# The first mixer's normalised input multiplied on VectorE instead of GpSimd, and 17 zero matmuls instead of 14 at the start

## The chip, the core and the metric

The kernel runs on one core of a Trainium2 chip. A core has five engines with a queue of instructions each: TensorE for matrix products (its weight loads are shown as a row of their own), VectorE, ScalarE and GpSimd for element-wise work, and SyncE, whose queue here issues DMAs. Each engine works through its queue in order and waits on semaphores for the others. The metric is the time of one execution on the device in microseconds (us); lower is better.

## The reference, cut to what matters

Two layers of a streaming encoder run over 320 tokens: 256 of a new stream and 64 of a running one. Layer 0 is a Mamba-2 mixer and a ConvFFN, layer 1 is an attention mixer and a ConvFFN. The change touches the way into the mixer of layer 0:

```python
def rmsnorm(x, g):
    xf = x.astype(F32)
    y = xf * lax.rsqrt(jnp.mean(xf * xf, axis=-1, keepdims=True) + EPS)
    return (y * g.astype(F32)).astype(x.dtype)

def mamba2_mixer(h, conv_buf, ssm_state, w_in, conv_w, conv_b, ...):
    zxbcdt = h @ w_in
    z, xbc, dt = jnp.split(zxbcdt, [D_INNER, D_INNER + CONV_DIM], axis=-1)
    xbc_c, new_buf = causal_dwconv(xbc, conv_buf, conv_w, conv_b)
    xbc_c = jax.nn.silu(xbc_c)
...
h = rmsnorm(x, norm_mix_pre[layer])
mix = mamba2_mixer(h, ...)
```

Here `x` has 1024 channels, and `w_in` is a 1024 x 5152 matrix. All numbers are float32.

## The kernel before, in words

**Layout.** Channels lie on the 128 partitions and the 320 tokens on the free axis, so `x` is eight tiles of 128 x 320, called k-blocks 0 to 7 here. One output block of a projection is 128 output channels: it is summed over the eight k-blocks in one PSUM bank.

**Three products for one.** Each float32 operand is split into a high part (rounded to the TensorE's fp32r type, on ScalarE) and a low part (the rest, on VectorE). A product is three matmuls: high by high, high by low, low by high (`mm3`, L279 and L280). A triple of them below means one k-block of one output block. Weights are split the same way as they arrive: `wh` on ScalarE (L322, L325), `wl` on VectorE (L324, L326); both have rings of four buffers.

**Scaling early or late.** The norm's factor of a token, 1/sqrt(mean square), is known only when all of `x` has been squared and summed. So the first output blocks multiply the unnormalised `x * g`, split into `xgh` and `xgl`, and their results are multiplied by the factor afterwards. These are four blocks in `outer` (the first one is `dt`, the other three go to convolutions 0, 1 and 2) and three more in the loop `for i in range(3, 3 + RAW0)` (convolutions 3, 4 and 5; "raw blocks" 3, 4, 5 below). From then on every block multiplies the normalised input, split into `xnh` and `xnl`.

**The normalised input.** `normalized` returns eight steps, one for each k-block. A step multiplies `x[:, k, :]` by the factor (`xr`, spread over the partitions) on GpSimd (L478), and splits the result `xn`, with the gain, on ScalarE (`xnh`, L325) and VectorE (`xnl`, L326). The tile `xn` has two buffers, so step k + 2 can start when both readers of step k are done. Three steps stand in the program behind raw block 3, three behind raw block 4, two behind raw block 5.

**What holds PSUM.** In this part the pool `pm` has four banks (`PSM`, m=4). The block `dt` gives its bank back when L815 has multiplied it by the factor; each convolution block gives its bank back when L642 has multiplied it by the factor into `ext`. Both run on VectorE. The tile `ext` has three buffers; a buffer comes free when the three taps of its convolution (L649, VectorE) and the copies of its last columns (L643 and L644, GpSimd) have been done. The first normalised block takes the fourth bank; the second one takes the bank of raw block 3, and so on.

**Zero matmuls.** `busy` (L375) issues matmuls of zeros whose result nothing reads; `run` issues `WARM` of them at L617, before any weight has arrived.

**Order.** In this part nobody writes the order by hand. The tile framework runs its own estimate of durations over the program (`schedule_with_timeline_sim=True`, L1515) and puts each engine's instructions into a fixed queue: what is ready first in its estimate goes first, and among several that are ready the one that stands earlier in the program. The chip then follows these queues whatever the true durations are.

Of the kernel before, what the change touches and what calls it, by code (L numbers as in the profile page):

```python
# [12 lines left out]
ALU = mybir.AluOpType  # L13
# [13 lines left out]
# the mixer of layer 0: projections, and how many steps of the scan and of the gate go with each block of them  # L27
# [6 lines left out]
WARM = 14  # L34
BA, BB = (14, 14, 14, 0), (10, 10, 10, 0)
AHEAD = 1, 2
# what is split before each of the three boundaries: units of the ring, units in a pool of their own; high parts right past it
# [8 lines left out]
# of 1 / sqrt(u), u from 0.932 to 1.07: over w = RSU * u, (w * w + RS[0] * w + RS[1]) * (w * w + RS[2] * w + RS[3])  # L46
# [35 lines left out]
class Kern:  # L82
# [132 lines left out]
    def ahead(self, i, cap=None):  # L215
        """loads and splits for the units after i; until the boundary is passed, two of the next phase's at most"""
        if cap is None:
            cap = self.ends[0] + RING[3 - len(self.ends)] if self.ends else len(self.q)
        while True:
            if self.qd < min(len(self.q), i + self.LD + 1, self.qs + 3):  # L220
                self._dma(self.qd)
                self.qd += 1
            elif self.qs < min(self.qd, i + self.LS + 1, cap):
                self._split(self.qs)()
                self.qs += 1
            else:
                return

    def early_open(self):
        """the weights of a phase that are loaded and split in the phase before, in a pool of their own"""  # L230
        early = self.early[3 - len(self.ends)]
        self.est = ExitStack()
        pool = self.pool(self.est, "early", "right")
        self.eready = []
        raws = []

        def load(src, n):
            raws.append(self.t(self.wp, [P, 1024], "wr", bufs=3))
            self.nc.sync.dma_start(out=raws[-1][:, :n], in_=src)

        def split(n, g):
            h, l = (self.t(pool, [P, n], f"e{c}{n}", F32R, bufs=sum(e[1] == n for e in early)) for c in "hl")
            r = raws.pop(0)
            for c0, c1, sc in g or ((0, n, None),):
                self.split(h[:, c0:c1], l[:, c0:c1], r[:, c0:c1], sc)
            self.eready.append((h, l))

        loads = [lambda u=u: load(*u[:2]) for u in early]
        splits = [lambda u=u: split(*u[1:]) for u in early]
        if loads:  # L250
            loads.pop(0)()
        return [(loads.pop(0) if loads else None, f) for f in splits]
# [8 lines left out]
    def high_ahead(self, n):  # L261
        """past the boundary: the high parts of the next units, and the low ones for later"""
        self.lows = []
        for _ in range(n):
            self.ahead(self.wi, self.qs)
            self.lows.append(self._split(self.qs))
            self.qs += 1
# [26 lines left out]
    def psum(self, **n):  # L294
        """the eight banks, by use"""
        if self.pst is not None:
            self.pst.close()
        self.pst = ExitStack()
        self.psp = {}
        for k, b in n.items():  # L300
            p = self.pst.enter_context(self.tc.tile_pool(name=self.nm("ps" + k), bufs=b, space=PSUM, reuse_waits="tile"))
            self.psp[k] = p
# [15 lines left out]
    def split_high(self, hdst, ldst, src, scale=None, pool=False):  # L318
        """the high part of src (by scale), and what makes the low one"""
        nc = self.nc  # L320
        if scale is None:
            self.high_ins = nc.scalar.activation(out=hdst, in_=src, func=AF.Copy).ins  # L322
            e = nc.gpsimd if pool else nc.vector
            return lambda: e.tensor_tensor(out=ldst, in0=src, in1=hdst.bitcast(F32), op=ALU.subtract)  # L324
        nc.scalar.activation(out=hdst, in_=src, func=AF.Copy, scale=scale)  # L325
        return lambda: nc.vector.scalar_tensor_tensor(out=ldst, in0=src, scalar=scale, in1=hdst.bitcast(F32),  # L326
                                                      op0=ALU.mult, op1=ALU.subtract)
# [4 lines left out]
    def newton(self, v, pool, tag):  # L332
        """1 / sqrt(v) of a few columns: a seed from the exponent, and a polynomial of fourth degree in v * seed ** 2"""
# [15 lines left out]
    def mean(self, src, dim, pool):  # L349
        """src / dim + eps"""  # L350
        v = self.t(pool, [P, 3], "nwv", bufs=3)
        self.nc.vector.tensor_scalar(v, src, 1.0 / dim, EPS, op0=ALU.mult, op1=ALU.add)
        return v

    def toksum(self, acc, ps, o=0):
        """sums over the channels, tokens on partitions: three columns (the last block twice)"""
        mm = self.nc.tensor.matmul
        one = self.ones[:, 0:1]
        for b in range(2):
            mm(ps[:, o + b:o + b + 1], acc[:, b * 128:b * 128 + 128], one, start=True, stop=True)  # L360
        for p0 in (0, 64):
            i = mm(ps[p0:p0 + 64, o + 2:o + 3], acc[:, 256:320], one, start=True, stop=True)
        self.pe_end = i.ins

    def spread(self, r, ps=None):
        """[tokens on partitions, 3] to every partition, tokens on the free axis (PSUM)"""
# [5 lines left out]
    def busy(self, ps, n, w=256):  # L372
        """matmuls of zeros, into columns that nothing reads: the array's clock drops when it rests for some microseconds"""
# [17 lines left out]
    def late_rstd(self):  # L391
        """of the eight output blocks: the sum of seven is there before the eighth"""
# [14 lines left out]
    def enter(self, xgp, sp, tag, g=None, boundary=True):  # L407
        """closes the residual of the layer before and splits x * g (block 0: x), channel block by block;
        sums the squares of x"""
# [60 lines left out]
    def normalized(self, xgp, sp, g, rstd):  # L470
        """x * rstd * g, in eight steps"""
# [4 lines left out]
        def step(k):  # L476
            xn = self.t(sp, [P, T], "xn", bufs=2)
            nc.gpsimd.tensor_tensor(out=xn, in0=self.x[:, k, :], in1=rstd, op=ALU.mult)  # L478
# [43 lines left out]
    def square_part(self, xh, xl, kbs, ps, mid, nstop):  # L522
        """a part of the sum of four output blocks of a 2048 x 1024 product, K outermost, two K blocks a unit"""
# [9 lines left out]
    def square_first(self, xh, xl, groups, ps, mid=None):  # L533
        """the first four output blocks of a 2048 x 1024 product, K outermost"""
# [27 lines left out]
    def outer_part(self, ps, ks, xh, xl, behind=None, turned=False):  # L562
        """K blocks of several output blocks; turned: block by block"""
# [14 lines left out]
    def outer(self, nblk, xh, xl, xacc, pool):  # L578
        """the first blocks of a projection, K outermost, and 1 / sqrt of the mean square of x"""
# [49 lines left out]
    def conv(self, ps, rstd, pool, k, pads, w, b, rows_out, dst=None):  # L629
        """k-tap depthwise conv along the tokens of both streams; returns (taps sum, ext)"""  # L630
# [22 lines left out]
    def after(self, ins, *earlier):  # L653
        """issue order alone"""
# [3 lines left out]
    def table(self, func):  # L658
        """has the table of a function loaded before it is waited for"""
# [13 lines left out]
    def ssm(self):  # L673
# [3 lines left out]
        with ExitStack() as st:  # L677
# [3 lines left out]
            with ExitStack() as s2:  # L681
# [4 lines left out]
                with ExitStack() as s3:  # L686
# [17 lines left out]
                    xnh, xnl, steps = self.normalized(xgp, dp, "mix_pre0", rstd)  # L704
# [97 lines left out]
    def ssm_dt(self, ps, rstd, sp, dp):  # L802
        """dt = softplus(.) and the sums of dt * a along a chunk; chunks and heads on partitions, tokens of a chunk on the free axis"""
# [60 lines left out]
    def ssd_select(self, g, sp):  # L864
        """X, of a pair of heads of the group and zero elsewhere, for the four pairs"""
# [4 lines left out]
    def ssd_decay(self, g, sp):  # L870
        """exp(acs_l - acs_s) under the causal mask, and exp(acs) by channel, of the heads of a group"""
# [136 lines left out]
    def ffn(self, i):  # L1008
        nc, a = self.nc, self.a
        with ExitStack() as st:  # L1010
# [3 lines left out]
            with ExitStack() as s2:  # L1014
# [9 lines left out]
                xnh, xnl, steps = self.normalized(xgp, sp, f"ffn_pre{i}", rstd)  # L1024
# [39 lines left out]
    def mla(self):  # L1064
        nc, a = self.nc, self.a
        tt, ts, stt = nc.vector.tensor_tensor, nc.vector.tensor_scalar, nc.vector.scalar_tensor_tensor
        with ExitStack() as st:
# [10 lines left out]
            with ExitStack() as s2:  # L1078
# [28 lines left out]
                # the norm of a projection of the normalized x, of its sums over the unscaled x: r / sqrt(mean * r * r + eps),  # L1107
                # r = 1 / sqrt(vx), is 1 / sqrt(mean + eps * vx)
# [80 lines left out]
    def turn_rope(self, sp, ps):  # L1189
        """the turned parts of two heads, of each the high rows and (in the rows of the other) the low ones; of the second the sample's tokens first"""  # L1190
# [32 lines left out]
    def attend(self, kp, sp, ql, kk, ch, cl, cqh, cql, sc, oh, ol, u):  # L1223
# [6 lines left out]
        def scores(qlh, qll, qs):  # L1230
            pt = self.t(sp, [P, 2, 3, 128], "pt", bufs=1)
            pss = self.t(sp, [P, T], "pss", bufs=2)
            for qb in range(3):
                ps = self.px()
                if qb == 0:
                    # the two parts of the keys side by side, their products added after
# [148 lines left out]
def _blocks(w):  # L1385
    """(K, N) to (N/128, 128, K/128 * 128): per output block, K rows on partitions"""
# [4 lines left out]
def _outer(w, nb):  # L1391
    """the first nb output blocks, K outermost: (8, 128, nb * 128)"""
# [3 lines left out]
def _square(w):  # L1396
    """(2048, 1024) to units in the order of use: 2 K blocks by 4 output blocks, then 8 K blocks of one"""
# [122 lines left out]
```

## Time and profile before

| what | value |
|---|---|
| median of the runs | 1015.43 us |
| lowest and highest of three runs | 1014.97 and 1017.46 us |
| span of the profiled execution | 1015.3 us |
| TensorE busy (matmul) | 987.5 us, 97% |
| VectorE busy | 753.6 us, 74% |
| ScalarE busy | 612.3 us, 60% |
| GpSimd busy | 352.3 us, 35% |

Only the span of the profiled execution is given, from its first to its last instruction; it lies 0.1 us under the median of the runs, so what lies around the span is smaller than the spread of the runs. In the rows of the profile PE is TensorE's matmuls, PEld its weight loads, DVE VectorE, ACT ScalarE, POOL GpSimd and SP SyncE. `L478` is line 478 of the kernel. In a timeline row the two first numbers are the start and the duration in us, and square brackets hold the idle time of that engine just before and the instruction that ended it.

### The profile page before, as it was taken

The page shows a single profiled execution, that of the slowest core. Times are in us where ns is not written, and L with a number is a line of the kernel's source. Part 1 is how long each engine was busy: PE and PEld are TensorE (multiplying, and loading weights), DVE is VectorE, ACT ScalarE, POOL GpSimd, SP SyncE. Part 2 cuts the span into 40 slices and gives each one's busy share as a digit, 9 for nine tenths or more (in the row PEclk, how much of TensorE's full clock was granted, in tenths as well). Part 3 has the DMA queues.
Part 4 walks back from the last instruction along what each step waited for, and adds up shares of the span by engine and source line. Part 5 has one row for each costly group of instructions (what it writes and reads, how often), then busy time and mean ns, then how long its engine had stood idle before and what let it go on. Part 6 is the DMA issues. An engine that isn't in the chain of part 4 may idle for free.

```text
span 1015.3 us, 18255 instructions
## 1 busy us (share of the span) xinstructions
PE 987.5 (97%) x6679; PEld 941.0 (93%) x6679; DVE 753.6 (74%) x1418; ACT 612.3 (60%) x1269; POOL 352.3 (35%) x601
## 2 busy tenths in 40 slices
PE   8999999999999999999999999999999999999995
PEld 7998888889988999999998899989999999999995
DVE  7896879767577999785447898886547999876333
ACT  7575777754455678665445487675545678665330
POOL 4832323000015676440005565640003667442001
PEclk9999999999999999999999999999999999999998
DMA  7352323233324344445641222232451444444441
GB/s 257 109 175 88 133 94 129 94 119 125 130 63 155 135 161 154 146 145 195 193 144 47 75 81 64 65 104 75 149 161 59 150 167 166 146 149 151 149 117 52
DMA packets 42664, 128.70 MB, mean 127 GB/s; under 512 B 4880, under 2 KB 8528, under 8 KB 42576
## 3 DMA queue, kind: packets, MB, share of 16 engines
q1 hardware_dynamic: 42288, 127.22, 37.9%
q8 instruction: 52, 0.85, 0.3%
q14 instruction: 36, 0.29, 0.1%
q10 hardware_dynamic: 288, 0.33, 0.1%
HBM read 123.46 MB, written 4.07 MB: 126 GB/s over the span
## 4 chain that ended last, share of the span: by engine, by line
PE 86%; DVE 8%; POOL 2%; issue 2%; ACT 1%; DMA 0%; DVEq 0%; POOLq 0%; ACTq 0%
PE pm L279 49%; PE pm L280 24%; PE px L279 2%; PE px L943 1%; PE px L960 1%; PE px L280 1%; DVE wl L324 1%; PE pb L886 1%; PE px L951 1%; POOL xacc L442 1%; PE pr L360 1%; POOL xn L478 1%; DVE y L450 1%; DVE x L454 1%; PE px L926 1%
## 5 line engine op out<-in xcount | busy, mean ns | idle before, releaser
L324 DVE TENSOR_TENSOR wl<-wr,wh 128x1024 fp32r<-128x1024 f32 (+2 forms) x204 | 246.8, 1210 | 119.5 <-ACT wh L322 114.4
L322 ACT ACTIVATE wh<-wr 128x1024 fp32r<-128x1024 f32 (+4 forms) x235 | 228.0, 973 | 163.5 <-PE pm L279 148.3
L279 PE MATMUL pm<-xnh,wh 128*128 128x320 f32 x784 | 244.7, 313 | 2.1 <-ACT xnh L325 1.8
L279 PE MATMUL pm<-xnl,wh 128*128 128x320 f32 x784 | 244.4, 312 | 0.3 <-DVE xnl L326 0.3
L280 PE MATMUL pm<-xnh,wl 128*128 128x320 f32 x784 | 244.3, 312 | 0.0
L279 PEld LDWEIGHTS pm<-xnh,wh 128*128 128x128 f32 x784 | 147.7, 189 | 5.8 <-issue 2.7
L280 PEld LDWEIGHTS pm<-xnh,wl 128*128 128x128 f32 x784 | 147.7, 189 | 3.5 <-issue 3.2
L279 PEld LDWEIGHTS pm<-xnl,wh 128*128 128x128 f32 x784 | 147.8, 189 | 3.2 <-issue 2.3
L279 PE MATMUL pm<-ah,wh 128*128 128x320 f32 x452 | 140.2, 311 | 0.0
L280 PE MATMUL pm<-ah,wl 128*128 128x320 f32 x452 | 140.1, 311 | 0.0
L279 PE MATMUL pm<-al,wh 128*128 128x320 f32 x452 | 139.9, 310 | 0.0
L649 DVE SCALAR_TENSOR_TENSOR cv<-ext,vec,cv 128x322 f32<-128x322 f32 x176 | 97.5, 568 | 5.5 <-ACT cv L647 3.0
L643 POOL COPY fsave<-ext 128x2 f32<-128x2 f32 x88 | 72.2, 821 | 53.8 <-ACT ext L640 49.3
L279 PEld LDWEIGHTS pm<-ah,wh 128*128 128x128 f32 x452 | 84.8, 188 | 1.2 <-ACT wh L322 0.8
L280 PEld LDWEIGHTS pm<-ah,wl 128*128 128x128 f32 x452 | 84.8, 188 | 0.5 <-issue 0.4
L279 PEld LDWEIGHTS pm<-al,wh 128*128 128x128 f32 x452 | 84.9, 188 | 0.1
L324 POOL TENSOR_TENSOR wl<-wr,wh 128x512 fp32r<-128x512 f32 (+2 forms) x31 | 43.5, 1418 | 103.6 <-ACT wh L322 100.6
L636 POOL MEMSET ext<- 128x2 f32 (+1 forms) x112 | 10.9, 98 | 188.7 <-PE px L943 55.9
L280 PE MATMUL pm<-xgh,wl 128*128 128x320 f32 x220 | 68.2, 314 | 0.7 <-DVE wl L326 0.7
L279 PE MATMUL pm<-xgl,wh 128*128 128x320 f32 x220 | 68.2, 313 | 0.3 <-DVE xgl L426 0.3
L279 PE MATMUL pm<-xgh,wh 128*128 128x320 f32 x220 | 63.1, 319 | 2.9 <-ACT xnh L325 1.4
L442 POOL TENSOR_TENSOR xacc<-xacc,xsq 128x320 f32<-128x320 f32 x28 | 29.2, 1043 | 104.3 <-ACT xsq L441 103.8
(424 smaller groups left out, 2200.7 us busy)
## 6 DMA issues: line engine op xcount, KB each, us to landing
wr<-w_up SPq DMA_DIRECT2D x76, 512.0 KB, 3.2
wr<-w_in SPq DMA_DIRECT2D x37, 512.0 KB, 3.3
wr<-w_dn SPq DMA_DIRECT2D x32, 512.0 KB, 3.5
wr<-w_out SPq DMA_DIRECT2D x16, 512.0 KB, 3.2
wr<-w_o SPq DMA_DIRECT2D x16, 512.0 KB, 3.2
wr<-w_up_k SPq DMA_DIRECT2D x16, 384.0 KB, 3.0
wr<-w_dn SPq DMA_DIRECT2D x16, 384.0 KB, 3.1
wr<-w_uq SPq DMA_DIRECT2D x8, 384.0 KB, 3.1
```

What stands on the lines that cost most here:

```text
L279: for i in (mm(out, wh, xh, start=first, stop=False), mm(out, wh, xl, start=False, stop=False), mm(out, wl, xh, start=False, stop=last)):
L280: mm(out, wl, xh, start=False, stop=last)):
L322: self.high_ins = nc.scalar.activation(out=hdst, in_=src, func=AF.Copy).ins
L324: return lambda: e.tensor_tensor(out=ldst, in0=src, in1=hdst.bitcast(F32), op=ALU.subtract)
L360: mm(ps[:, o + b:o + b + 1], acc[:, b * 128:b * 128 + 128], one, start=True, stop=True)
L442: nc.gpsimd.tensor_tensor(out=acc, in0=acc, in1=s, op=ALU.add)
L450: tt(out=yk, in0=yk, in1=r, op=ALU.mult)
L454: e.tensor_tensor(out=xk, in0=xk, in1=yk, op=ALU.add)
L478: nc.gpsimd.tensor_tensor(out=xn, in0=self.x[:, k, :], in1=rstd, op=ALU.mult)
L636: nc.gpsimd.memset(ext[:, 0:m], 0.0)
L643: nc.gpsimd.tensor_copy(out=rows_out[:, 0, :], in_=ext[:, TP:TP + m])
L649: nc.vector.scalar_tensor_tensor(out=c, in0=ext[:, i:i + n], scalar=w(i), in1=c, op0=ALU.mult, op1=ALU.add)
```

## The change

Two edits change what is computed where; the others in the diff take comments out.

```diff
-WARM = 14
+WARM = 17
...
-    def normalized(self, xgp, sp, g, rstd):
+    def normalized(self, xgp, sp, g, rstd, e):
...
-            nc.gpsimd.tensor_tensor(out=xn, in0=self.x[:, k, :], in1=rstd, op=ALU.mult)
+            e.tensor_tensor(out=xn, in0=self.x[:, k, :], in1=rstd, op=ALU.mult)
...
-                    xnh, xnl, steps = self.normalized(xgp, dp, "mix_pre0", rstd)
+                    xnh, xnl, steps = self.normalized(xgp, dp, "mix_pre0", rstd, nc.vector)
...
-                xnh, xnl, steps = self.normalized(xgp, sp, f"ffn_pre{i}", rstd)
+                xnh, xnl, steps = self.normalized(xgp, sp, f"ffn_pre{i}", rstd, nc.gpsimd)
```

In the first layer's mixer all eight multiplications of `x` by the factor go to VectorE. The two ConvFFNs keep theirs on GpSimd. `run` issues 17 zero matmuls instead of 14.

## The prediction

> **What bounds the kernel now.** I read the page first: its span, the busy shares and the row of slices.
>
> ```profile
> span 1015.3 us, 18255 instructions
> PE 987.5 (97%) x6679; PEld 941.0 (93%) x6679; DVE 753.6 (74%) x1418; ACT 612.3 (60%) x1269; POOL 352.3 (35%) x601
> PE   8999999999999999999999999999999999999995
> ```
>
> TensorE (PE) is busy nearly all the time, so a microsecond comes off the total only where PE stands still or runs slowly, and from there a gain is carried to the end as long as no later wait takes it back. The first two slices (25 us each) hold the first mixer's entry. Next I read the chain of work that ended last, for the first 60 us (start, us, what).
>
> ```profile
> 27.22 1.77 issue
> ...
> 29.01 3.73 issue
> 32.74 0.53 POOL ssave L644
> 33.27 1.67 POOL xn L478 x2
> ...
> 35.36 4.13 POOL xn L478
> ...
> 39.52 0.57 ACT xnh L325
> ...
> 40.13 1.16 PE pm L279 x3
> ```
>
> From 27 to 40 us the chain runs through GpSimd (POOL): a copy of three columns, then the steps that the change moves, then `xnh`, and only then PE. The timeline of that stretch shows why, and what PE does meanwhile.
>
> ```profile
> 27.09 5.70 POOL L643 COPY ssave<-ext 128x3 f32<-128x3 f32 x1
> 38.05 0.31 PE L280 MATMUL pm<-xnh,wl 128*128 128x320 f32 x1
> 40.13 0.90 PE L279 MATMUL pm<-xnh,wh 128*128 128x320 f32 x2 [1.77 <-ACT xnh L325]
> 41.09 0.47 PE L280 MATMUL pm<-xnh,wl 128*128 128x320 f32 x1
> 41.36 0.47 PE L279 MATMUL pm<-xnh,wh 128*128 128x320 f32 x1
> 43.76 0.37 PE L279 MATMUL pm<-xnh,wh 128*128 128x320 f32 x1
> ```
>
> A copy of 128x3 took 5.70 us, while VectorE (DVE) had no gap. The tile view gives the moved instruction the same spread:
>
> ```profile
> L478 POOL TENSOR_TENSOR xn<-x,xr x8: 870/946/4124, 23.0 to 43.0; 128x320 f32<-128x320 f32 x8
> ```
>
> Alone it takes 0.87 us, at worst 4.12. The Trainium skill, page "SBUF — State Buffer", section "SBUF: two separate sides", says that GpSimd and a VectorE instruction with two SBUF inputs exclude each other for a whole instruction; these rows agree with it.
>
> PE waited 1.77 us at 38.3 and then ran at half speed: 0.27 us from one matmul to the next (41.09 to 41.36) until 43.76. The windows view (window, length, then busy us and count of PE, PEld, DVE, ACT, POOL, then PE's granted clock, DMA share and GB/s) gives the full pace and the load of VectorE.
>
> ```profile
> 22.00:48.00 26.00, 22.78 (x141) 21.99 (x140) 22.71 (x49) 14.69 (x25) 22.09 (x25) 0.93 0.41 142
> 25.80:36.40 10.60, 10.60 (x72) 10.60 (x73) 9.09 (x23) 5.45 (x9) 9.51 (x9) 1.00 0.43 151
> 36.40:43.76 7.36, 5.59 (x28) 5.23 (x26) 5.64 (x12) 4.29 (x8) 7.33 (x14) 0.78 0.21 73
> ```
>
> 72 matmuls in 10.60 us are 0.147 us each: three raw blocks without a gap. In the third window PE did 25 (28 less three at the edges), which need 25 x 0.147 = 3.7 us; 3.7 of 7.4 us are lost there.
>
> **The change part by part.**
>
> *Taking `xn` off GpSimd.* Gone are eight instructions and the wait for them, and one stretched weight split:
>
> ```profile
> 21.89 1.08 DVE L324 TENSOR_TENSOR wl<-wr,wh 128x896 fp32r<-128x896 f32 x1
> 22.95 2.69 POOL L478 TENSOR_TENSOR xn<-x,xr 128x320 f32<-128x320 f32 x2 [5.13 <-ACT xr L388]
> 23.16 1.76 DVE L324 TENSOR_TENSOR wl<-wr,wh 128x896 fp32r<-128x896 f32 x1
> 24.84 0.81 DVE L815 TENSOR_TENSOR v<-pm,xr 32x128 f32<-32x128 f32 x3
> 25.80 0.39 PE L279 MATMUL pm<-xgh,wh 128*128 128x320 f32 x1 [1.45 <-ACT xnh L325]
> ```
>
> The same split takes 1.08 us alone and 1.76 beside `xn`. Behind it stands L815, which frees the PSUM bank that raw block 3 needs; the profile names `xnh` as releaser, but the block reads no `xnh`, and L815 ends at 25.65. So raw block 3 can start 0.68 us earlier, and the raw blocks end at about 35.75 instead of 36.43.
>
> *Putting it on VectorE.* The nearest row is a two-input instruction of the same shape; the pitch in a full queue comes from two neighbours.
>
> ```profile
> 5.10 0.48 DVE L429 TENSOR_TENSOR xgl<-x,xgh 128x320 fp32r<-128x320 f32 x1
> 35.34 0.54 DVE L649 SCALAR_TENSOR_TENSOR xs<-ext,vec,xs 128x323 f32<-128x323 f32 x1
> 35.80 0.54 DVE L326 SCALAR_TENSOR_TENSOR xnl<-xn,vec,xnh 128x320 fp32r<-128x320 f32 x1
> ```
>
> 0.46 us from start to start: eight steps are 8 x 0.46 = 3.7 us. In 22 to 48 us VectorE had 26.0 - 22.7 = 3.3 us free, and 0.68 us more comes from the split above: the steps fit, with almost nothing over. What matters is what they are put ahead of. Behind them stand the low parts `xnl`, the weight splits, the `dt` arithmetic, the convolution taps, and L642, which empties the banks:
>
> ```profile
> 34.73 0.55 DVE L326 SCALAR_TENSOR_TENSOR xnl<-xn,vec,xnh 128x320 fp32r<-128x320 f32 x1 [1.51 <-ACT xnh L325]
> 39.76 0.54 DVE L642 TENSOR_TENSOR ext<-pm,xr 128x256 f32<-128x256 f32 x2
> 45.07 0.54 DVE L642 TENSOR_TENSOR ext<-pm,xr 128x256 f32<-128x256 f32 x2
> ```
>
> L642 at 39.76 gives back the bank of raw block 3 at B = 40.30. The second normalised block needs it. PE reaches it when the first normalised block is done: 35.75 + 24 x 0.147 = 39.3. So once `xn` is no longer late, the next thing that is late is this bank. Before it VectorE had one gap of 1.51 us. The inputs of `xn` are complete at 22.9, before anything that the raw blocks bring, so I let all eight stand ahead of L642. Then B = 40.30 + 3.7 - 1.51 - 0.68 = 41.8. The four `xnl` that came after it before may move ahead too: 4 x 0.46 = 1.8 more, B = 43.6. If the planner puts L642 no later than now, B = 40.3 or less. I take 41.8, the middle one, since two steps may be in flight at a time and `xnl` waits for ScalarE in between.
>
> *What it is worth.* Before, PE had done 25 normalised matmuls by 43.76. After, it has done 24 by B and goes on at 0.147 us. The gain is therefore (43.76 - B) - 0.147, if the clock holds: 1.8 us for B = 41.8, 3.3 for 40.3, 0 for 43.6, and 43.76 - 39.3 - 0.15 = 4.3 without any wait.
>
> *The clock.* The wait for B = 41.8 is 2.5 us in one piece, longer than the 1.77 behind which it fell. Against a fall speaks the full work of 36.4 to 39.3 before it, where the old profile had 38.36 - 36.4 = 2.0 us of work. A fall costs what it cost before: 43.76 - 40.13 = 3.6 us at half speed, so 1.7 us. I take no fall.
>
> *The zero matmuls.*
>
> ```profile
> 1.05 3.17 PE L375 MATMUL pb<-warm 128*128 128x256 bf16 x14 [1.05 <-DVE warm L614]
> 4.81 1.44 PE L571 MATMUL pm<-xgh,wh 128*128 128x320 f32 x4 [0.59 <-ACT xgh L419]
> 6.04 1.27 PE L571 MATMUL pm<-xgh,wl 128*128 128x320 f32 x4
> ...
> 14.71 1.17 DVE L426 SCALAR_TENSOR_TENSOR xgl<-x,vec,xgh 128x320 fp32r<-128x320 f32 x1
> ...
> 16.51 0.31 PE L279 MATMUL pm<-xgl,wh 128*128 128x320 f32 x1
> ...
> 18.05 0.48 PE L885 MATMUL pb<-maskr,idr 128*128 128x512 f32 x1 [0.20 <-DVE maskr L798]
> ```
>
> 14 take 3.17 us, 0.226 each, and PE then idles 0.59 us for `xgh`; three more fill 0.68 us, so the first real matmul comes at most 0.1 us later. If they also bring the clock up sooner, PE gets ahead by some tenths only: the low part of k-block 5 is ready at 15.88 and used at 16.51, so 0.63 us is all that VectorE allows there, and at 18.05 PE waits for VectorE anyway. Bounds: 0.1 lost to 0.6 gained. I take 0, since the factor's chain runs through VectorE.
>
> *Later.* TensorE's turn of `w` is the first place where the gain may be given back.
>
> ```profile
> 59.46 0.29 DVE L848 TENSOR_TENSOR w<-w,dt 96x128 f32<-96x128 f32 x1 [0.71 <-ACT w L669]
> ...
> 61.69 0.14 PEld L851 LDWEIGHTS px<-con,w 96*128 96x128 f32 x1
> ```
>
> `w` is there 1.9 us before its use: a gain of 1.8 just fits, a larger one needs the `dt` arithmetic earlier as well. The sum: span 1015.3 - 1.8 = 1013.5; the median stands 0.1 over the span, so **1013.6**.
>
> **The rivals.**
>
> *A, VectorE's queue is put in good order.* B is 40.3 or less: gain 3.3 to 4.2. For it: the queue is written by readiness, and the bank's instruction stands earlier in the program than `xn`. Against it: `w` has 1.9 us. Time 1011.2 to 1012.1; I write 1011.6.
>
> *B, the bank takes the whole gain.* All `xn` and `xnl` stand ahead of L642: B = 43.6, gain 0, time 1015.4. For it: two instructions of each step are ready in turn, and VectorE had only 3.3 us free.
>
> *C, slower: the bank comes so late that the clock falls again.* With B = 43.6 PE stands still for 4.3 us, more than twice the old wait, and then runs at half speed for 3.6 us: 1.7 us lost, 1017.1; if raw block 4's bank, next in the same queue, makes it fall a second time, 1018.8. It decides from B of about 43. For it: the 1.77 us that were enough before. The Trainium skill, page "Perfetto Trace Analysis", section "Optimizing Scalar/DVE Operations", would rather have work taken off a saturated VectorE, which is this side of the matter.
>
> *D, the clock comes up early at the start.* PE gets 0.6 us ahead in the front and keeps it in `xn`'s stretch: 1013.6 - 0.6 = 1013.0. The Trainium skill, page "TensorE: Matmul & The Clock Gate", Part 1, asks for about 3.4 us of sustained work before the full clock; by that rule 14 zero matmuls (3.17 us) are short of it and 17 are not. The row at 6.04, four matmuls in 1.27 us, agrees that 14 didn't do; whether 17 do no run here shows yet. Against more than 0.6: VectorE, as above.
>
> *E, the change doesn't do what it says* would need PE's wait at 40.13 to have another cause than `xn`. The chain ends POOL at 39.49 and starts `xnh` at 39.52, so I give it no share of its own.
>
> **How the numbers follow.** Forecast 1013.6: 0.38. A: 0.25. B: 0.15. C: 0.12. D: 0.10. About 0.3% (3.05 us) is what a measurement of this kernel can tell from no change: faster means under 1012.4, slower over 1018.5. Faster: most of A (0.22) and the low ends of the forecast and of D (0.07), 0.29. Slower: the double fall in C (0.06), and 0.04 from a new order elsewhere, since the planner writes all queues again; 0.10. Same: 0.61. The range goes from A's low end less the 0.5 us by which the lowest run lies under the median, 1010.7, to C's single fall, 1017.1.
>
> **What would show it right or wrong.** Right: no `xn` on POOL; the eight on DVE at about 0.48 us each; the split at 23.16 near 1.08; raw block 3 starting near 25.1; PE's one wait in 35 to 44 us is for DVE L642 or an `xnl`, and ends near 41.8; pace 0.147 behind it. The clock's part: look whether matmuls follow each other by 0.147 or 0.27 us right behind the wait, and how soon after 4.81 the pace reaches 0.147. Wrong: PE waits for `xn` on DVE itself (the steps were put too late in its queue); a new wait at `w` near 60 us or beyond; more than 1 us moved in the front; or a wait after 290 us that the old profile doesn't have, from the new order.

## The result, and the profile after

The changed kernel takes 1021.54 us (median of 5 runs, 1020.28 to 1022.38). The kernel before, run beside it, takes 1017.16 us (5 runs, 1014.97 to 1017.51). In the 21 to 27 runs beside the experiments its median is 1015.91 to 1016.35, and its executions differ with the clock: those with a mean granted clock of 0.991 or more span less than 1014.9 us, those with 0.989 or 0.990 span 1014.9 us or more. The ratio is 1.0053 (the two medians alone would give 1.0043), with a 95% interval of 1.0040 to 1.0066: the change makes the kernel slower by half a per cent, some 5 us. The profiled execution of the changed kernel took 1022.38 us, and its span is 1020.6 us, so 1.8 us lie around the span.

The page of the changed kernel: the span, the engines' busy time, the slices of PE and of the clock that it was granted.

```profile
span 1020.6 us, 18260 instructions
...
PE 990.3 (97%) x6682; PEld 942.6 (92%) x6682; DVE 755.1 (74%) x1426; ACT 611.5 (60%) x1269; POOL 348.8 (34%) x593
...
PE   8989999999999999999999999999999999999995
...
PEclk9989999999999999999999999999999999999998
```

Third slice, 51 to 77 us: both rows show an 8. The old profile had a 9 in its row of PE there. The windows view prices the 25 us around it (window and length, then busy us and count of PE, PEld, DVE, ACT, POOL, then granted clock, DMA share, GB/s). First the kernel before:

```profile
25.00:50.00 25.00, 22.43 (x140) 22.10 (x141) 21.71 (x51) 13.64 (x24) 21.94 (x27) 0.93 0.33 116
50.00:75.00 25.00, 25.00 (x171) 24.31 (x170) 23.23 (x46) 18.66 (x38) 9.54 (x20) 1.00 0.49 162
```

The changed kernel, same windows:

```profile
25.00:50.00 25.00, 23.47 (x145) 22.82 (x146) 25.00 (x61) 14.82 (x25) 23.50 (x22) 0.93 0.36 120
50.00:75.00 25.00, 22.11 (x122) 20.04 (x122) 18.90 (x37) 16.25 (x34) 4.92 (x11) 0.86 0.42 137
```

Up to 50 us PE does five matmuls more, at the price that VectorE (DVE) has no idle time left: 25.00 of 25.00 us. From 50 to 75 us PE stands still for 2.9 us and its clock falls to 0.86; before, it was busy throughout. From 75 to 100 us PE is busy throughout again (25.00 of 25.00 us). The change was meant for the first of these stretches; the loss is in the second.

**The first stretch.** PE's timeline of the changed kernel (start, duration, in brackets the idle time before and what ended it):

```profile
25.07 0.39 PE L279 MATMUL pm<-xgh,wh 128*128 128x320 f32 x1 [0.75 <-DVE v L815]
...
35.71 0.31 PE L279 MATMUL pm<-xnh,wh 128*128 128x320 f32 x1
...
38.06 0.41 PE L279 MATMUL pm<-xnl,wh 128*128 128x320 f32 x1 [0.53 <-DVE xnl L326]
...
39.54 0.39 PE L279 MATMUL pm<-xnh,wh 128*128 128x320 f32 x1 [0.93 <-DVE ext L642]
...
40.22 0.47 PE L279 MATMUL pm<-xnh,wh 128*128 128x320 f32 x1
40.49 0.47 PE L279 MATMUL pm<-xnl,wh 128*128 128x320 f32 x1
...
43.65 0.31 PE L279 MATMUL pm<-xnh,wh 128*128 128x320 f32 x1
```

Only 12 normalised matmuls stand ahead of the wait for the bank, not 24. VectorE's timeline shows why:

```profile
25.43 0.88 DVE L478 TENSOR_TENSOR xn<-x,xr 128x320 f32<-128x320 f32 x2
...
38.86 0.54 DVE L642 TENSOR_TENSOR ext<-pm,xr 128x256 f32<-128x256 f32 x2
...
40.45 0.48 DVE L478 TENSOR_TENSOR xn<-x,xr 128x320 f32<-128x320 f32 x1
...
45.51 0.88 DVE L478 TENSOR_TENSOR xn<-x,xr 128x320 f32<-128x320 f32 x2
```

Four `xn` (two of them at 31.48 and 33.02, not shown) stand ahead of the bank's L642 and four behind it (one at 41.05, not shown). With only four k-blocks ready, PE's queue leaves the first block half done, goes to the second one and finds its bank occupied until 39.40. Between 35.71 and 43.65 PE does 29 normalised matmuls, worth 29 x 0.147 = 4.3 us of 7.9: it loses 3.7 us there, as much as before. What is won in this stretch is what raw block 3 brought along, 0.7 us (35.71 against 36.43).

**The second stretch.** PE of the changed kernel, 54 to 64 us:

```profile
54.25 0.30 PE L851 MATMUL px<-con,w 96*128 96x96 f32 x1 [0.49 <-DVE w L848]
...
56.75 0.53 PE L860 MATMUL px<-alast,par 64*128 64x96 f32 x2 [1.80 <-DVE alast L857]
57.88 0.64 PE L280 MATMUL pm<-xnh,wl 128*128 128x320 f32 x1 [0.60 <-DVE wl L324]
58.31 0.47 PE L279 MATMUL pm<-xnh,wh 128*128 128x320 f32 x1
...
63.38 0.47 PE L279 MATMUL pm<-xnl,wh 128*128 128x320 f32 x1
...
64.18 0.31 PE L279 MATMUL pm<-xnh,wh 128*128 128x320 f32 x1
```

Three waits for VectorE, 0.49 + 1.80 + 0.60 = 2.9 us, and then half pace: 20 matmuls from 58.31 to 63.38 start 0.267 us apart instead of 0.147, 2.4 us more. The longest wait is for `alast`. On VectorE and GpSimd, changed kernel, and then the tile view of `alast` (min/median/max in ns, first and last start):

```profile
54.01 2.36 POOL L867 TENSOR_TENSOR xp<-X,con 64x1280 fp32r<-64x1280 f32 x1 [3.55 <-PE pm L280]
...
54.11 2.58 DVE L857 TENSOR_SCALAR alast<-con,X 64x32 fp32r<-64x32 f32 x3
```

```profile
L857 DVE TENSOR_SCALAR alast<-con,X x3: 223/226/2294, 54.1 to 56.5; 64x32 fp32r<-64x32 f32 x3
```

The same instructions in the kernel before:

```profile
62.98 0.52 DVE L857 TENSOR_SCALAR alast<-con,X 64x32 fp32r<-64x32 f32 x3
...
65.06 0.42 PE L860 MATMUL px<-alast,par 64*128 64x96 f32 x2
...
66.47 2.31 POOL L867 TENSOR_TENSOR xp<-X,con 64x1280 fp32r<-64x1280 f32 x1
```

Two things have moved. PE's queue now asks for `w` at 54 us instead of 62 and for `alast` at 55 instead of 65. Counted in normalised matmuls that stand ahead of them, `w` has moved from 147 to 96 and `alast` from 167 to 98: 51 and 69 matmuls, 7.5 and 10.1 us at full pace. VectorE has `w` done at 54.19 instead of 59.75, sooner than before, but not by as much as PE asks for it sooner. And GpSimd's `xp` (L867), which came after `alast`, now starts beside it. Three instructions of 0.23 us then take 2.58 us: the first of them takes 2.29.

The sum is 2.9 + 2.4 - 0.7 = 4.6 us of the 5.3 by which the spans differ. Most of the rest lies in how a wait is counted. The brackets count from the modelled end of a matmul, 0.31 us after its start, while at full pace the next one starts 0.147 us after it. From start to start the three waits cost 3.4 us (0.73, 1.87 and 0.77), and the matmuls from 57.88 to 64.18 take 2.8 us too long; less the 0.7 won, that is 5.5. All of the loss arises in the mixer. The place where PE sums the squares of its output over the channels shows it, in the kernel before and then in the changed one:

```profile
287.32 0.58 PE L360 MATMUL pr<-ones,yacc 128*128 128x1 f32 x4 [0.39 <-DVE yacc L500]
```

```profile
292.53 0.58 PE L360 MATMUL pr<-ones,yacc 128*128 128x1 f32 x4 [0.38 <-DVE yacc L500]
```

PE is 5.2 us late there, and 5.3 at the end.

The theory to test: VectorE, full since 25 us, finishes the `dt` arithmetic too late for the new place of `w` and `alast`; `xp` beside `alast` makes it much later; and the wait that this makes also costs the clock. The rivals: the zero matmuls do it; the new place on PE alone does it; VectorE's lateness does it wherever those instructions stand.

### The profile page after: what moved, and what is told of

It reads as the page before. It is cut to its first block, busy times and chain, and to the rows that moved or that the text cites. A ratio compares the mean times of both kernels' runs of the same rounds, so it can differ in the third digit from the quotient of the medians.

```text
span 1020.6 us, 18260 instructions
## 1 busy us (share of the span) xinstructions
PE 990.3 (97%) x6682; PEld 942.6 (92%) x6682; DVE 755.1 (74%) x1426; ACT 611.5 (60%) x1269; POOL 348.8 (34%) x593
## 4 chain that ended last, share of the span: by engine, by line
PE 86%; DVE 8%; issue 2%; POOL 2%; ACT 1%; DMA 0%; SPq 0%; DVEq 0%; POOLq 0%; ACTq 0%
PE pm L279 49%; PE pm L280 24%; PE px L279 2%; PE px L943 1%; DVE wl L324 1%; PE px L960 1%; PE px L280 1%; PE pb L886 1%; PE px L951 1%; POOL xacc L442 1%; PE pr L360 1%; DVE y L450 1%; DVE x L454 1%; PE px L926 1%; PE pr L369 0%
```

## The experiments

### Which of the two edits: e1_warm17 and e2_xn_only

The kernel before with 17 zero matmuls, and the changed kernel with 14.

```diff
 e1_warm17, on the kernel before
-WARM = 14
+WARM = 17
 e2_xn_only, on the kernel after
-WARM = 17
+WARM = 14
```

> The kernel before with 17 zero matmuls instead of 14, xn still on GpSimd. Theory (the loss comes from xn on VectorE, by the new order that it brings): the front moves by less than 0.5 us, the rest of the queues stay as before, so the time is that of before within 1 us (ratio 0.999 to 1.001). Rival (the zero matmuls cost it): 3 us or more over before.

> The changed kernel with 14 zero matmuls: xn on VectorE alone. Theory: the whole loss is there, 4 to 6 us over before (ratio 1.004 to 1.006), with TensorE's waits for w (L851), alast (L860) and wl between 54 and 58 us as in the changed kernel. Rival (zero matmuls): within 1 us of before.

e1_warm17: 1016.77 us beside 1016.11, ratio 1.0008 [0.9999, 1.0018]. e2_xn_only: 1022.17 us, ratio 1.0066 [1.0051, 1.0081]. The whole loss belongs to the multiplications on VectorE; the three zero matmuls alone change nothing that can be told. In e2_xn_only PE waits 1.50 us for `w`, 1.80 for `alast` and 0.47 for `wl`, with the clock at 0.86 from 50 to 75 us: the same picture. One thing differs. The waits of 0.53 and 0.92 us near 39 us are there too, but the clock holds behind them (granted clock 1.00 from 25 to 50 us). PE does 151 matmuls in that window, 11 more than before, which is a lead of 1.6 us; and it spends this lead at `w`, which VectorE has ready at the same time: that wait ends at 54.34, in the changed kernel at 54.25. So the half pace near 40 us costs the changed kernel next to nothing in the end: L360 of `yacc` starts at 292.53 there and at 292.32 in e2_xn_only.

e1_warm17 shows something else. Its PE waits for `xnh` as the kernel before does; its timeline, and its window:

```profile
40.23 0.70 PE L279 MATMUL pm<-xnh,wh 128*128 128x320 f32 x2 [1.78 <-ACT xnh L325]
40.76 0.31 PE L279 MATMUL pm<-xnl,wh 128*128 128x320 f32 x1
40.91 0.31 PE L280 MATMUL pm<-xnh,wl 128*128 128x320 f32 x1
```

```profile
25.00:50.00 25.00, 22.26 (x147) 21.67 (x148) 21.72 (x52) 13.66 (x24) 21.94 (x27) 1.00 0.35 120
```

The wait is 1.78 us, where it was 1.77, and the pace behind it is 0.147 us, where it was 0.27. One and the same wait costs the clock in one execution and doesn't in another. The span of this execution is 1013.0 us instead of 1015.3, but not all of that is this fall: PE reaches L360 of `yacc` at 286.18 instead of 287.32, 1.1 us sooner. Another 1.1 us come right behind it, where the next 14 zero matmuls (L375) take 1.70 us here and 3.07 in the profiled execution of the kernel before, half pace again.

### xp away from alast: e6_xp_late

The changed kernel; GpSimd's first `xp` is queued behind the copies of the next convolution block. It is issue order alone.

```diff
-        nc.gpsimd.tensor_copy(out=rows_out[:, 1, :], in_=ext[:, W - m:W])
+        self.copied = nc.gpsimd.tensor_copy(out=rows_out[:, 1, :], in_=ext[:, W - m:W]).ins
...
+                            if g == 1 and i == 0:
+                                self.after(self.xp0, self.copied)
...
```

> The changed kernel with TensorE's order up to that point kept, but GpSimd's xp product (L867, 2.36 us) is queued behind the column copies of the next block, so that it no longer runs beside VectorE's alast (L857). Theory of the shared access (xp keeps alast waiting: 2.58 us for three instructions that took 0.52): the three take about 0.6 us again, the wait at L860 falls from 1.8 to under 0.3 us, the clock holds, 3.5 to 5 us less than the changed kernel. Rival (VectorE is simply late with the dt part): alast is fast, but the wait at L860 or for wl right behind it stays over 1 us and the clock falls, less than 2 us won.

Measured: 1017.23 us, ratio 1.0015 [1.0005, 1.0025]. Against the changed kernel's 1.0053 that is 0.0038 x 1016 = 3.9 us back. `xp` starts at 62.0 us. PE's timeline (lines are two higher here: L853 is L851, L862 is L860), and the tile view of `alast` (min/median/max in ns, first and last start):

```profile
54.65 0.30 PE L853 MATMUL px<-con,w 96*128 96x96 f32 x1 [0.48 <-DVE w L850]
...
55.28 0.42 PE L862 MATMUL px<-alast,par 64*128 64x96 f32 x2
56.21 0.41 PE L280 MATMUL pm<-xnh,wl 128*128 128x320 f32 x1 [0.51 <-DVE wl L324]
56.46 0.31 PE L279 MATMUL pm<-xnh,wh 128*128 128x320 f32 x1
56.60 0.31 PE L279 MATMUL pm<-xnl,wh 128*128 128x320 f32 x1
```

```profile
L859 DVE TENSOR_SCALAR alast<-con,X x3: 225/225/226, 54.5 to 54.8; 64x32 fp32r<-64x32 f32 x3
```

The matmuls of `w` and `alast` stand as early as in the changed kernel. `alast` takes 0.225 us each, nothing waits at L862, and the pace is 0.147 us. The two smaller waits stay, 1.0 us together, and the clock outlives them. By the rows, 1.9 us of waits and 2.4 us of half pace are gone, 4.3 in all, near the 3.9 measured. Trace against trace it is 3.8: PE reaches L360 of `yacc` at 288.69 instead of 292.53.

### The clock's share alone: e8_fill

The changed kernel with 16 zero matmuls between the last L851 and L860; the collision stays.

```diff
...
+        self.pe_end = e
+        self.busy(pc, 16)
         for odd in range(2):
-            nc.tensor.matmul(pc[:, 0:96], self.par[:, 128 * odd:128 * odd + 128], al, start=odd == 0, stop=odd == 1)
+            i = nc.tensor.matmul(pc[:, 0:96], self.par[:, 128 * odd:128 * odd + 128], al, start=odd == 0, stop=odd == 1).ins
+            self.after(i, self.pe_end)
```

> The changed kernel with 16 zero matmuls between TensorE's last turn of the dt part (L851) and L860, where it waits for alast. They fill the wait and shorten nothing: xp still runs beside alast. Theory (the wait of about 2.3 us at L860 costs itself and, because the clock falls behind it, some 2.5 us more): L860 starts as late as in the changed kernel, the matmuls behind follow by 0.147 us, and 2 to 2.5 us are won, 1019 to 1019.8 where before is 1016. Rival (the wait alone is the price): less than 0.7 us won.

Measured: 1019.11 us beside 1016.35, ratio 1.0027 [1.0018, 1.0037]. PE's timeline (L862 is L860 here):

```profile
54.47 1.91 PE L375 MATMUL px<-warm 128*128 128x256 bf16 x16
56.76 0.42 PE L862 MATMUL px<-alast,par 64*128 64x96 f32 x2 [0.37 <-DVE alast L857]
...
58.29 0.31 PE L279 MATMUL pm<-xnl,wh 128*128 128x320 f32 x1
58.44 0.31 PE L280 MATMUL pm<-xnh,wl 128*128 128x320 f32 x1
```

The matmul of `alast` starts at 56.76, as late as in the changed kernel (56.75), and `alast` is still stretched. Behind it the pace is 0.147 us. It is worth (1.0053 - 1.0027) x 1016 = 2.6 us by the medians, give or take some 1.6 by their intervals; the rows of the changed kernel say 2.4, and so do the two traces, in which PE reaches L360 of `yacc` at 290.12 instead of 292.53. Of the 3.8 us that e6_xp_late wins by the same mark, the half-pace spell is thus more than half. Near 40 us the clock held in this execution, as in e2_xn_only, and the wait for `w` took the lead. Two reservations: the planner's order behind L860 is another one here, and in four of the ten executions the mean granted clock was 0.987, as low as in the changed kernel, so the fill may not have kept the pace in all of them.

### The old order back: e3_dt_late and e7_dt_back

e3_dt_late puts PE's L851 and L860 of the changed kernel behind the second convolution block of group 1. e7_dt_back does that, queues ScalarE's exponentials for `w` behind the four copies of `z`, and `xp` behind that block's copies.

```diff
 e3_dt_late
+                            if g == 1 and i == 1:
+                                for d in self.dtpe:
+                                    self.after(d, self.mm_end)
...
 e7_dt_back, besides
...
+                                self.after(self.xp0, self.copied)
...
+                            if g == 0 and i == 3:
+                                for d in self.wexp:
+                                    self.after(d, j)
```

> The changed kernel, but TensorE's five instructions of the dt part (L851 three times, L860 twice) are put behind the second block of convolution group 1 in its queue, about where they stood before. Theory (the new order asks for them two blocks, 7 us, earlier than VectorE can have them): no wait at L851 or L860, no half clock near 58 us, 5 us less than the changed kernel, 1015 to 1016.5 where before is 1016. Rival (VectorE is overloaded by eight more instructions whatever the order): TensorE waits for wl or L642 in the same stretch instead, less than 2 us won.

> The changed kernel with the dt part put back on three engines: ScalarE's exponential of w behind the four copies of z, TensorE's turns and L860 behind the second block of convolution group 1, GpSimd's xp behind that block's column copies. xn stays on VectorE. Theory (the loss is the dt part's place, not xn's cost on VectorE): no wait of TensorE over 0.6 us between 44 and 70 us, time that of before within 1.5 us, and below the variant in which TensorE alone was put back (1.0027 of before). Rival (VectorE is overloaded by xn): waits for wl or for L642 stay, and the time stays 2.5 us or more over before.

e3_dt_late: 1018.76 us, ratio 1.0027 [1.0015, 1.0039], half of the loss back. It doesn't isolate PE's order: the planner moved `xp` as well, to 61.72, and the three `alast` take 0.52 us together. Even so PE waits 1.65 us for a bank that ScalarE's copy of `z` frees, 0.98 us for `wl`, and runs at half pace again. e7_dt_back: 1019.73 us, ratio 1.0032 [1.0020, 1.0044]. That was to cure it and did not. PE's timeline, and VectorE's (L866 is L857 here):

```profile
55.58 0.41 PE L280 MATMUL pm<-xnh,wl 128*128 128x320 f32 x1 [2.41 <-DVE wl L324]
...
56.93 0.47 PE L279 MATMUL pm<-xnl,wh 128*128 128x320 f32 x1
57.20 0.47 PE L280 MATMUL pm<-xnh,wl 128*128 128x320 f32 x1
```

```profile
54.16 0.23 DVE L866 TENSOR_SCALAR alast<-con,X 64x32 fp32r<-64x32 f32 x1
54.32 1.21 DVE L324 TENSOR_TENSOR wl<-wr,wh 128x1024 fp32r<-128x1024 f32 x1
```

With the `dt` matmuls out of the way PE meets the next thing that VectorE is late with, the low part of a weight block that stands behind the `dt` arithmetic: one wait of 2.41 us, and half pace behind it. This is the third rival, and it is partly right. The place of the `dt` part decides which late instruction PE meets; VectorE being late is there in either order. What e6_xp_late does better is that PE waits 1.0 us in all instead of 2.4, in two pieces of half a microsecond, and the pace behind them was full.

### alast on ScalarE, and half of the steps: e4_alast_act and e5_half

```diff
 e4_alast_act, on the kernel after
-            ts(al[:, c * 32:c * 32 + 32], self.c("esel")[0:64], X[0:64, l0 + n - 1:l0 + n].bitcast(F32), None, op0=ALU.mult)
+            nc.scalar.activation(out=al[:, c * 32:c * 32 + 32], in_=self.c("esel")[0:64], func=AF.Copy, scale=X[0:64, l0 + n - 1:l0 + n].bitcast(F32))
 e5_half, on the kernel after
-            e.tensor_tensor(out=xn, in0=self.x[:, k, :], in1=rstd, op=ALU.mult)
+            (e if k >= KD // 2 else self.nc.gpsimd).tensor_tensor(out=xn, in0=self.x[:, k, :], in1=rstd, op=ALU.mult)
```

> The changed kernel with alast made on ScalarE instead of VectorE; xp stays where it is. A second way to take alast out of xp's way: ScalarE shows no stretching beside GpSimd in any row so far. Theory of the shared access: 3 us or more won over the changed kernel, no wait for alast. Rival (the place of the dt part alone): TensorE waits as long, for alast from ScalarE. The planner also moves L860 some 30 matmuls back here, so that this run alone does not decide.

> Only k-blocks 4 to 7 of xn on VectorE, 0 to 3 stay on GpSimd; 17 zero matmuls. The planner leaves the dt part on TensorE more than a block later than in the changed kernel. Theory (the dt part's place decides): no wait for alast, within 2 us of before, if TensorE's wait at the fourth k-block goes, up to 3 us under it. Rival (each xn on VectorE costs): half of the changed kernel's loss, 2.5 us over before.

e4_alast_act: 1017.75 us beside 1016.35, ratio 1.0008 [0.9999, 1.0017]. e5_half: 1016.84 us, ratio 1.0006 [0.9996, 1.0015]. Neither isolates one cause, because the planner's order changed with each: PE's L860 stands at 60.32 in the one and at 61.03 in the other, and waits for nothing there. They show that all eight multiplications on VectorE need not be slower (e4_alast_act has all eight there), and that with four of them nothing is won either: PE waits 1.72 us for `xnh` at 38.3 in e5_half.

### Filling the wait near 40 us: e9_before_fill and e10_xp_fill

After e8_fill the question was whether the half-pace spell near 40 us, which both kernels have, can be bought off. In e9_before_fill 14 zero matmuls stand behind the 12th normalised matmul of the kernel before; in e10_xp_fill 10 stand at that place in e6_xp_late.

```diff
         for k in range(KD):
...
+            if self.nblock == RAW0 + 1 and k == 3:
+                self.pe_end = self.last
+                self.busy(self.pr(), 14)
+                behind = self.pe_end
...
```

> The kernel before (xn on GpSimd, 14 zero matmuls at the start), with 14 more zero matmuls of 256 columns behind the 12th matmul of the first normalised block and ahead of everything that follows it on TensorE. Theory (a wait in one piece costs its length and then a spell at half pace): the 1.77 us wait for xnh at 38.4 us is filled (14 x 0.11 = 1.5 us), the pace behind it stays 0.147 us, and of the 1.8 us that the spell cost (29 us of span less) about 1.5 come back in a run whose clock fell before: about 1.0 to 1.7 us under the kernel before, 0 where its clock had not fallen. Rival (the clock falls for another reason, or the new order spends the gain): the pace behind the fill is 0.27 us again or a new wait stands between 45 and 75 us, and the time is within 0.5 us of before or over it.

> The kernel after with GpSimd's xp behind the copies (as in e6_xp_late) and 10 zero matmuls behind the 12th matmul of the first normalised block. Theory: the half pace of 40 to 43.4 us goes (about 13 matmuls x 0.12 = 1.5 us), so 1.5 us under e6_xp_late, which makes it about as fast as before or up to 0.5 us faster. Rival (VectorE is the bound of this stretch): what TensorE wins at 40 us it waits for again between 50 and 60 us, for wl, w or a bank, and the time is that of e6_xp_late or higher, 1.0010 to 1.0030 of before.

e9_before_fill: 1015.09 us beside 1015.91 (11 and 21 runs), ratio 0.9989 [0.9980, 0.9999]. e10_xp_fill: 1015.54 us, ratio 0.9995 [0.9986, 1.0004]. PE's timeline of e9_before_fill (L376 is L375 here, L326 is L325):

```profile
37.74 1.70 PE L376 MATMUL pr<-warm 128*128 128x256 bf16 x14
39.68 0.70 PE L279 MATMUL pm<-xnh,wh 128*128 128x320 f32 x2 [0.24 <-ACT xnh L326]
40.22 0.31 PE L279 MATMUL pm<-xnl,wh 128*128 128x320 f32 x1
40.37 0.31 PE L280 MATMUL pm<-xnh,wl 128*128 128x320 f32 x1
```

The pace behind the fill is full in both. That alone proves little, since the pace near 40 us was full in e1_warm17 and e2_xn_only without a fill. For e9_before_fill all executions speak: none of the eleven has a mean granted clock under 0.991, while six of the 21 of the kernel before have 0.989. With `xn` left on GpSimd it is the fastest kernel of this study by a little, 0.8 us under the kernel before where 1.0 to 1.7 was expected: the interval ends just under 1, and among ten kernels that is no firm difference. e10_xp_fill is 0.0020 x 1016 = 2.0 us better than e6_xp_late, where 1.5 was expected; but its `dt` matmuls also came later in the new order (`w`'s and `alast`'s at 60.2 and 60.6 us, without a wait). e2_xn_only shows that a held clock near 40 us alone only lengthens the wait for `w`, so the new place of `w` probably matters more than the fill; no run separates the two. I can't say that the one of the two is better than the other.

## Why the prediction was wrong

The forecast was 1013.6 us and a gain of 1.8; the kernel took 1021.54 us and lost about 5, outside the range. By the prediction's own steps:

- *The split and raw block 3*: right. The split at 23.12 takes 1.08 us, raw block 3 starts at 25.07 (forecast 25.1), the profile now names L815 as its releaser, and the raw blocks end at 35.71 (35.75).
- *Eight steps on VectorE*: right. Eight at 0.48 us, and VectorE full; "with almost nothing over" was true, and I drew too little from it.
- *The bank*: wrong in its parts. I put all eight ahead of L642 and had PE reach the bank after 24 matmuls with B = 41.8. Four came behind it; B was 39.40; PE reached it after 12 matmuls, because its queue goes to the second block once four k-blocks are done. The gain came out at 0.7 us instead of 1.8 in this execution. In e2_xn_only and e8_fill, where the clock held, it was 1.6 us at 50 us, close to the forecast; with two waits of 0.5 and 0.9 us in place of the one of 2.5 that the sum had, that agreement is luck.
- *No fall of the clock there*: wrong in this execution, where PE ran at half pace until 43.4 behind waits of 0.53 and 0.93 us. Behind the same two waits it kept the full pace in the profiled executions of e2_xn_only, e3_dt_late, e7_dt_back and e8_fill, so a choice between the two wasn't to be had from one trace. The price was too high as well: 1.7 us in the prediction, 1.1 us left at the mixer's end between e1_warm17 and the kernel before.
- *Zero matmuls at 0*: right (1.0008 [0.9999, 1.0018]). Rival D was right in its condition and not in its effect. The front of the changed kernel's timeline:

```profile
1.05 3.81 PE L375 MATMUL pb<-warm 128*128 128x256 bf16 x17 [1.05 <-DVE warm L614]
...
5.90 0.75 PE L571 MATMUL pm<-xgh,wl 128*128 128x320 f32 x4
...
18.01 0.47 PE L885 MATMUL pb<-maskr,idr 128*128 128x512 f32 x1 [0.60 <-DVE maskr L798]
```

  Four matmuls take 0.75 us at 5.90 where they took 1.27: the clock is up sooner. Three more matmuls aren't needed for that in every execution, though: in e9_before_fill 14 zero matmuls take 3.03 us and the first four real ones 0.86. At 18.01 PE waits 0.60 us for VectorE instead of 0.20, as the prediction said it would, and the lead is gone.
- ***Later*: this is the step that failed.** I took `w`'s place in PE's queue from the old profile, gave it a slack of 1.9 us and asked whether a gain of 1.8 fits. That place wasn't fixed. The planner wrote it 51 matmuls forward and `alast`'s 69, into the stretch where VectorE was latest, and GpSimd's `xp` beside `alast`. I had named it ("a new order elsewhere, since the planner writes all queues again") and given it a chance of 0.04, as a mishap without place or price. It had both: PE stood still for 0.49 us at `w`, 1.80 at `alast` and 0.60 at `wl`, and ran at half pace behind them. e6_xp_late prices the collision of `xp` and `alast` with the clock's fall at 3.9 us, e8_fill the fall alone at 2.6. Why the planner moved them I did not see: its estimates are in no trace.
- *0.1 us around the span*: wrong. The changed kernel's profiled execution has 1.8 us around its span. The old span of 1015.3 was of an execution with a fallen clock, set beside a median of others; e1_warm17's 1013.0 is a span without that fall and without the one near 290 us. The forecast was about 1.7 us too low from that alone, an estimate from these rows.

Of the 1.5 us by which e6_xp_late stays over the kernel before, 1.4 are there at L360 of `yacc` (288.69 against 287.32); its two waits, for `w` and for `wl`, cost 1.3 us from start to start. So VectorE's lateness for the new places of `w` and `wl` remains as the likely rest; no run takes it away with nothing else changed. Open is why the planner chose the new order.

## What to carry to other kernels

Work put on an engine that is nearly full doesn't only delay what is queued behind it there: if a planner writes the queues, list what the other engines need from the filled engine for the next 30 us, and ask of each what it costs if it is asked for several microseconds earlier. Before giving GpSimd less to do, look where its long instructions will go instead, because beside a short VectorE instruction that TensorE waits for, one of them can cost nearly its whole length (here 2.29 us beside 2.36). And price a TensorE wait with the half-pace spell that may follow; in the profiled executions of the three kernels here that fill a wait with 10 to 16 zero matmuls, the pace behind it was full.

## What the runs showed of the hardware

- A TENSOR_SCALAR of 64x32, 0.23 us alone, took 2.29 us beside GpSimd's `xp` (2.36 us), and ended when `xp` did. The Trainium skill, page "SBUF — State Buffer", section "SBUF: two separate sides", says that one of the two engines holds the shared access for a whole instruction and the other is blocked fully; the row agrees. The page names VectorE instructions with two SBUF inputs or in a two-port mode; which of these this one is, no run here shows.
- Of two waits at the same place the one of 1.77 us halved the pace (kernel before) and the one of 1.78 us did not (e1_warm17). Two waits of 0.53 and 0.93 us within 2.0 us halved it in the changed kernel, e4_alast_act and e6_xp_late (granted clock 0.93 from 25 to 50 us) and left it full in e2_xn_only, e3_dt_late, e7_dt_back and e8_fill (1.00). One of 2.41 us halved it (e7_dt_back); two of 0.48 and 0.51 us within 2.0 us did not (e6_xp_late). The Trainium skill, page "TensorE: Matmul & The Clock Gate", Part 1, has the clock judged over windows of about 3.4 us that run freely of the program, and fall after an idle window. Free-running windows agree with the two outcomes of the same waits; a whole idle window was not needed.
- Half-pace spells lasted 3.4 us (39.96 to 43.36) and 3.6 us (40.13 to 43.76) near 40 us, but 5.9 us (58.31 to 64.18) in the second stretch of the changed kernel. By the granted clock the half speed itself lasted some 7 us there (0.14 x 25 / 0.5, from the 0.86 of that window) and 3.5 us near 40 us (0.07 x 25 / 0.5).
